# FFN gate tiles copied by DMA into float32r tiles and transposed in that type, with a later flip in the loop

## The chip, the cores and the metric

The kernel runs on one core of one Trainium2 chip, as one launch. The metric is the device time of a run in microseconds; the runs shown are the median of three. A profile is one execution recorded by the hardware profiler. TensorE (PE, with its weight loads as PEld) multiplies and transposes, VectorE (DVE) and ScalarE (ACT) work element by element, GpSimd (POOL) does small arithmetic and can issue DMAs, SyncE (SP) issues DMAs.

## The reference

A trunk of four residual layers over 256 tokens of 1024 numbers. Each layer has a token mixer (retention, a convolution module, dilated attention, retention again), then a SwiGLU feed-forward part. The change lies in the latter:

```python
def _swiglu(h, w_in, w_out):
    a = h @ w_in
    return (jax.nn.silu(a[..., :FFN_HIDDEN]) * a[..., FFN_HIDDEN:]) @ w_out

for i in range(DEPTH):
    ...                                  # token mixer m
    x = x + _rmsnorm(m, norm_w[i, 1])
    f = _swiglu(_rmsnorm(x, norm_w[i, 2]), ffn_w_in[i], ffn_w_out[i])
    x = x + _rmsnorm(f, norm_w[i, 3])
```

`FFN_HIDDEN` is 2816. All inputs and the output are float32.

## The kernel before

**Precision.** A float32 operand of a large matmul is split into two float32r tiles, a high part and the rest (`split`, lines 50 and 51: ACT casts the high part, DVE subtracts). Three float32r matmuls, high by high, high by rest and rest by high, stand for one float32 product. In the rows, `xTh`/`xTl` are the two parts of the transposed activations, `wh`/`wl` of the weights going up, `poolh`/`pooll` of the weights coming down, `fhh`/`fhl` of the transposed gate tiles.

**Tiling.** The tokens are two halves of 128 (t = 0, 1). The 2816 hidden columns are 11 groups (c) of 256. `proj` (line 183) makes one unit of "up": 24 matmuls of 512 columns (256 gate and 256 value columns) into the PSUM tile `mm`. It is divided into four steps s of 6 matmuls, and its argument `mid` can place other work ahead of a step. ACT then computes the silu of the gate half (line 448) and DVE multiplies it with the value half (line 450), both into the SBUF tile `fsg`.

**Flip.** The product has tokens on the partitions and must have hidden columns there for the next matmul. `flip` (line 459) does this on TensorE: two 128x128 transposes against the identity `ident`, into the PSUM tile `aux`, in float32. Behind it `split` writes `fhh` and `fhl`. `down` (line 200) then has 12 matmuls of 512 columns, which accumulate the output in `acc`. Per layer there are 22 units of up, flip and down, 88 in the kernel.

**Order.** The loop over c is written out by hand: up for group c + 1 of half 0, down for group c of half 0, flip of (0, c + 1), up for group c of half 1, down for group c - 1 of half 1, flip of (1, c). `FFN_HOLD` holds one `down` of half 1 back to the last round. A scheduler then orders the instructions of each engine, and may move a flip by some matmuls. `flush(t)` (line 162) transposes the normalised activations of a half; `finish` adds the result to the residual stream, and POOL computes the root mean squares in it (lines 110 to 113: `rs` of a result, `rsx` of the next input).

**Queues.** All DMAs are issued by SP. Weights come in loads of 512 KB into `raw`, which has 7 buffers. POOL's queue holds only its norm arithmetic. The identity is loaded once, at the start, into a float32 tile.

Of the kernel before, what the change touches and what calls it, by code (L numbers as in the profile page):

```python
# [8 lines left out]
F32 = mybir.dt.float32  # L9
F32R = mybir.dt.float32r  # L10
# [4 lines left out]
P = 128  # L15
# [9 lines left out]
WBUFS = 10  # L25
RAWBUFS = 7
FOBUFS = 6
FFN_HOLD = True
CONV_EARLY = 3
CONV_FENCE = 1  # L30
APE = 3
# [6 lines left out]
def tile_trunk(ctx: ExitStack, tc: tile.TileContext, a):  # L38
    nc = tc.nc

    const = ctx.enter_context(tc.tile_pool(name="const", bufs=1))
    wp = ctx.enter_context(tc.tile_pool(name="wp", bufs=WBUFS))
# [3 lines left out]
    def bank(tag):  # L46
        return ps.tile([P, 512], F32, tag=tag, name=tag, bufs=4 if tag == "acc" else 2)

    def split(h, l, src):
        ia = nc.scalar.copy(h, src)  # L50
        iv = nc.vector.tensor_sub(l, src, h.bitcast(F32))  # L51
        return ia, iv
# [9 lines left out]
    def load_w(src, cols=1024, pool=None, bufs=None):  # L62
        raw = wp.tile([P, 1024], F32, tag="raw", name="raw", bufs=RAWBUFS)
        nc.sync.dma_start(raw[:, :cols], src)
        if pool is None:
            h = wp.tile([P, 1024], F32R, tag="wh", name="wh")
            l = wp.tile([P, 1024], F32R, tag="wl", name="wl")
        else:
            h = pool.tile([P, 1024], F32R, tag="poolh", name="poolh", bufs=bufs)
            l = pool.tile([P, 1024], F32R, tag="pooll", name="pooll", bufs=bufs)  # L70
        cast[0], cast[1] = split(h[:, :cols], l[:, :cols], raw[:, :cols])
        return h, l
# [13 lines left out]
    nc.sync.dma_start(grow, a["norm_w"][0:1, :])  # L86
    for hh in range(2):
        nc.sync.dma_start(xs[0][:, hh * 512 : hh * 512 + 512], a["x"][0][:, hh * 512 : hh * 512 + 512])
    ident = const.tile([P, P], F32, tag="ident", name="ident")
    nc.sync.dma_start(ident, a["ident"])  # L90
    ones = const.tile([1, P], F32, tag="ones", name="ones")
    nc.vector.memset(ones, 1.0)
    gain0 = [bank("acc"), bank("acc")]
# [58 lines left out]
    def flush(t):  # L152
        if t not in todo:
            return
        xg = todo.pop(t)
        h = const.tile([P, KB, P], F32R, tag=f"xTh{t}", name=f"xTh{t}")
        l = const.tile([P, KB, P], F32R, tag=f"xTl{t}", name=f"xTl{t}")
        for hh in range(2):
            b = bank("aux")
            for k in range(4):  # L160
                kk = 4 * hh + k
                nc.tensor.transpose(b[:, k * P : (k + 1) * P], xg[:, kk * P : (kk + 1) * P], ident)
            split(
                h[:, 4 * hh : 4 * hh + 4, :].rearrange("p k t -> p (k t)"),
                l[:, 4 * hh : 4 * hh + 4, :].rearrange("p k t -> p (k t)"),
                b,
            )
        xTh[t], xTl[t] = h, l

    def proj(t, ws, width, out, mid=None):  # L170
        n = 0
        for s in range(4):
            if isinstance(mid, dict):
                if s in mid:
                    mid[s]()
            elif s == 2 and mid is not None:
                mid()
            wh, wl = ws[s]
            for kb in range(2):
                k = 2 * s + kb  # L180
                sl = slice(kb * width, (kb + 1) * width)
                for st, mv in ((xTh, wh), (xTh, wl), (xTl, wh)):
                    nc.tensor.matmul(out, lhsT=st[t][:, k, :], rhs=mv[:, sl], start=(n == 0), stop=(n == 23))  # L183
                    n += 1

    def out_block(acc, sth, stl, w, first, last, by_half=False):
        if by_half:
            for hh in range(2):
                for i, (st, mv) in enumerate(((sth, w[0]), (sth, w[1]), (stl, w[0]))):
                    nc.tensor.matmul(  # L190
                        acc[hh],
                        lhsT=st,
                        rhs=mv[:, hh * 512 : hh * 512 + 512],
                        start=(first and i == 0),
                        stop=(last and i == 2),
                    )
            return
        for i, (st, mv) in enumerate(((sth, w[0]), (sth, w[1]), (stl, w[0]))):
            for hh in range(2):
                nc.tensor.matmul(  # L200
                    acc[hh],
                    lhsT=st,
                    rhs=mv[:, hh * 512 : hh * 512 + 512],
                    start=(first and i == 0),
                    stop=(last and i == 2),
                )
# [228 lines left out]
    def ffn_first(i):  # L435
        return [load_w(a["ffn_w_in"][i, 0, s]) for s in range(4)]
# [3 lines left out]
    def ffn(i, finish, pool):  # L440
        st = {}
        acc = {}

        def up(t, c, mid=None):
            b = bank("mm")
            proj(t, st["w", c], 512, b, mid)
            sg = pool.tile([P, 256], F32, tag="fsg", name="fsg", bufs=3)
            nc.scalar.activation(sg, b[:, 0:256], AF.Silu, scale=rsx[t])  # L448
            sm = sg
            nc.vector.scalar_tensor_tensor(  # L450
                out=sm, in0=b[:, 256:512], scalar=rsx[t], in1=sg, op0=ALU.mult, op1=ALU.mult
            )
            st["s", t, c] = sm

        def flip(t, c):
            sm = st["s", t, c]
            tp = bank("aux")
            for k in range(2):
                nc.tensor.transpose(tp[:, k * P : (k + 1) * P], sm[:, k * P : (k + 1) * P], ident)  # L459
            hh = pool.tile([P, 2, P], F32R, tag="fhh", name="fhh", bufs=4)  # L460
            hl = pool.tile([P, 2, P], F32R, tag="fhl", name="fhl", bufs=4)
            split(hh.rearrange("p a b -> p (a b)"), hl.rearrange("p a b -> p (a b)"), tp[:, 0:256])
            st["h", t, c] = (hh, hl)

        def down(t, c, mid=None):
            if c == 0:
                acc[t] = [bank("acc"), bank("acc")]
            hh, hl = st["h", t, c]
            for k in range(2):
                if k and mid is not None:  # L470
                    mid()
                out_block(
                    acc[t],
                    hh[:, k, :],
                    hl[:, k, :],
                    st["o", c][k],
                    c == 0 and k == 0,
                    c == FFN_GROUPS - 1 and k == 1,
                    by_half=(t == 1 and c == FFN_GROUPS - 1 and k == 1),
                )  # L480

        def wload(c):
            st["w", c] = [load_w(a["ffn_w_in"][i, c, s]) for s in range(4)]

        def oload(c):
            st["o", c] = [load_w(a["ffn_w_out"][i, 2 * c + k], pool=pool, bufs=FOBUFS) for k in range(2)]

        last = FFN_GROUPS - 1
        st["w", 0] = wnext.pop("w") if "w" in wnext else ffn_first(i)
        flush(0)  # L490
        up(0, 0)
        for c in range(FFN_GROUPS):
            if c < last:
                wload(c + 1)
                up(0, c + 1, {1: lambda: flip(0, 0), 2: lambda: flush(1)} if c == 0 else None)
            oload(c)
            down(0, c)
            if c < last:
                flip(0, c + 1)
            up(1, c)  # L500
            if c == last:
                finish(0, acc[0])
            if c == 1:
                flip(1, 0)
            if c == last and FFN_HOLD:
                down(1, c - 2)
            if c >= 1:
                if c != last - 1 or not FFN_HOLD:
                    down(1, c - 1, (lambda: flush(0)) if c == last else None)
                flip(1, c)  # L510
        down(1, last)
        finish(1, acc[1])

# [337 lines left out]
    for i in range(DEPTH):  # L851
# [3 lines left out]
        def finish(t, f):  # L855
            post_norm(t, f, gains[0])
            pre_norm(t, gains[1])
# [26 lines left out]
        with tc.tile_pool(name=f"ffn{i}", bufs=2) as pool:  # L884
            ffn(i, finish_ffn, pool)
# [95 lines left out]
```

## Time and profile before

| | before |
|---|---|
| median of 3 runs | 1611.8 us (1610.49 to 1613.36) |
| profiled execution, its own time | 1612.1 us |
| its span, first to last instruction | 1610.3 us |
| busy share PE / DVE / ACT / POOL | 99% / 64% / 54% / 4% |
| mean granted TensorE clock | 0.997 |
| moved by DMA | 274.27 MB, mean 170 GB/s |

The page shows busy times, the span in slices, DMA queues, the chain of work that ended last, and the costliest groups of instructions. A row of the timeline has the start in us, the length, the engine, the line, the operation, the tile written and the tiles read, shapes and a count; in brackets stands how long the engine sat idle before it and what ended that. The chain lists pieces as start, length, what. `x2` at a piece counts instructions.

### The profile page before, as it was taken

The page shows a single profiled execution, that of the slowest core. Times are in us where ns is not written, and L with a number is a line of the kernel's source. Part 1 is how long each engine was busy: PE and PEld are TensorE (multiplying, and loading weights), DVE is VectorE, ACT ScalarE, POOL GpSimd, SP SyncE. Part 2 cuts the span into 40 slices and gives each one's busy share as a digit, 9 for nine tenths or more (in the row PEclk, how much of TensorE's full clock was granted, in tenths as well). Part 3 has the DMA queues.
Part 4 walks back from the last instruction along what each step waited for, and adds up shares of the span by engine and source line. Part 5 has one row for each costly group of instructions (what it writes and reads, how often), then busy time and mean ns, then how long its engine had stood idle before and what let it go on. Part 6 is the DMA issues. An engine that isn't in the chain of part 4 may idle for free.

```text
span 1610.3 us, 20999 instructions
## 1 busy us (share of the span) xinstructions
PE 1589.4 (99%) x7742; PEld 1344.2 (83%) x7742; DVE 1038.5 (64%) x1576; ACT 864.4 (54%) x1376; POOL 71.3 (4%) x106
## 2 busy tenths in 40 slices
PE   9999999999999999999999999999999999999998
PEld 6888878888787888889999999788888888878886
DVE  7655685646797854567776767755657655675452
ACT  7544464545677644446665656644555444565341
POOL 1000010001000100010000000100011000010000
PEclk9999999999999999999999999999999999999999
DMA  8645465555304755444444444564555554475530
GB/s 315 230 140 186 155 236 184 199 193 183 122 1 138 255 201 191 160 139 144 148 146 139 145 147 158 186 226 164 203 178 166 188 167 138 157 248 194 198 118 27
DMA packets 79881, 274.27 MB, mean 170 GB/s; under 512 B 9377, under 2 KB 9633, under 8 KB 79778
## 3 DMA queue, kind: packets, MB, share of 16 engines
q1 hardware_dynamic: 79778, 272.92, 50.6%
q8 instruction: 61, 1.00, 0.2%
q14 instruction: 42, 0.34, 0.1%
HBM read 271.84 MB, written 1.05 MB: 169 GB/s over the span
## 4 chain that ended last, share of the span: by engine, by line
PE 90%; ACT 3%; DVE 2%; DMA 2%; issue 1%; POOL 1%; SPq 0%; DVEq 0%; POOLq 0%; ACTq 0%
PE mm L183 57%; PE acc L200 21%; PE acc L577 3%; PE acc L774 1%; PE aux L459 1%; PE aux L324 1%; PE acc L733 1%; PE acc L731 1%; PE aux L759 1%; ACT wh L50 1%; ACT junk L118 1%; DMA raw<-in_ffn_w_out 1%; DVE wl L51 1%; PE aux L300 1%; PE aux L695 1%
## 5 line engine op out<-in xcount | busy, mean ns | idle before, releaser
L183 PE MATMUL mm<-wh,xTh 128*128 128x512 f32 (+1 forms) x1536 | 591.1, 385 | 1.2 <-ACT xTh L50 1.2
L183 PE MATMUL mm<-wl,xTh 128*128 128x512 f32 (+1 forms) x1536 | 579.4, 377 | 0.0
L183 PE MATMUL mm<-wh,xTl 128*128 128x512 f32 (+1 forms) x1536 | 579.2, 377 | 0.0
L51 DVE TENSOR_TENSOR wl<-raw,wh 128x1024 fp32r<-128x1024 f32 (+1 forms) x432 | 497.3, 1163 | 116.8 <-ACT wh L50 102.9
L50 ACT CAST wh<-raw 128x1024 fp32r<-128x1024 f32 (+1 forms) x432 | 429.6, 1005 | 138.7 <-PE mm L183 103.6
L183 PEld LDWEIGHTS mm<-wh,xTl 128*128 128x128 f32 x1536 | 288.8, 188 | 45.8 <-DVE xTl L51 0.3
L183 PEld LDWEIGHTS mm<-wh,xTh 128*128 128x128 f32 x1536 | 289.0, 188 | 43.4 <-ACT xTh L50 1.6
L183 PEld LDWEIGHTS mm<-wl,xTh 128*128 128x128 f32 x1536 | 289.4, 188 | 41.9 <-DVE wl L51 0.5
L448 ACT ACTIVATE fsg<-mm,rsx 128x256 f32<-128x256 f32 x88 | 41.7, 474 | 169.0 <-PE mm L183 168.9
L450 DVE SCALAR_TENSOR_TENSOR fsg<-mm,rsx,fsg 128x256 f32<-128x256 f32 x88 | 42.3, 481 | 124.8 <-ACT fsg L448 124.7
L51 DVE TENSOR_TENSOR pooll<-raw,poolh 128x1024 fp32r<-128x1024 f32 x88 | 107.3, 1222 | 7.7 <-ACT poolh L50 7.0
L200 PE MATMUL acc<-poolh,fhh 128*128 128x512 f32 x344 | 107.6, 393 | 0.5 <-ACT fhh L50 0.5
L200 PE MATMUL acc<-poolh,fhl 128*128 128x512 f32 x344 | 107.2, 392 | 0.0
L200 PE MATMUL acc<-pooll,fhh 128*128 128x512 f32 x344 | 106.0, 389 | 0.0
L50 ACT CAST poolh<-raw 128x1024 fp32r<-128x1024 f32 x88 | 92.6, 1054 | 24.2 <-PE acc L200 14.6
L51 DVE TENSOR_TENSOR fhl<-aux,fhh 128x256 fp32r<-128x256 f32 x88 | 37.0, 421 | 98.6 <-ACT fhh L50 98.6
L50 ACT CAST fhh<-aux 128x256 fp32r<-128x256 f32 x88 | 32.5, 369 | 114.4 <-PE aux L459 114.4
L200 PEld LDWEIGHTS acc<-poolh,fhh 128*128 128x128 f32 x344 | 63.7, 188 | 15.1 <-ACT fhh L50 2.7
L200 PEld LDWEIGHTS acc<-pooll,fhh 128*128 128x128 f32 x344 | 64.6, 188 | 13.5
L200 PEld LDWEIGHTS acc<-poolh,fhl 128*128 128x128 f32 x344 | 64.3, 188 | 13.5
L561 DVE SCALAR_TENSOR_TENSOR cv<-upad,wdw,cv 128x256 f32<-128x256 f32 x143 | 59.5, 479 | 0.8
L110 POOL TENSOR_SCALAR rs<-ss 128x1 f32<-128x1 f32 x16 | 7.3, 455 | 1050.9 <-ACT junk L118 1050.9
(178 smaller groups left out, 1617.6 us busy)
## 6 DMA issues: line engine op xcount, KB each, us to landing
raw<-in_ffn_w_in SPq DMA_DIRECT2D x176, 512.0 KB, 4.9
raw<-in_ret_w_in SPq DMA_DIRECT2D x96, 512.0 KB, 4.8
raw<-in_ffn_w_out SPq DMA_DIRECT2D x88, 512.0 KB, 4.5
raw<-in_attn_w_in SPq DMA_DIRECT2D x96, 384.0 KB, 3.8
raw<-in_ret_w_out SPq DMA_DIRECT2D x32, 512.0 KB, 4.4
raw<-in_conv_w_in SPq DMA_DIRECT2D x16, 512.0 KB, 5.0
gain<-in_norm_w SPq DMA_DIRECT2D x15, 512.0 KB, 5.3
raw<-in_conv_w_out SPq DMA_DIRECT2D x8, 512.0 KB, 4.5
```

What stands on the lines that cost most here:

```text
L50: ia = nc.scalar.copy(h, src)
L51: iv = nc.vector.tensor_sub(l, src, h.bitcast(F32))
L118: nc.scalar.activation(junk, src, AF.Square, scale=scale, accum_out=acc)
L183: nc.tensor.matmul(out, lhsT=st[t][:, k, :], rhs=mv[:, sl], start=(n == 0), stop=(n == 23))
L200: nc.tensor.matmul(acc[hh], lhsT=st, rhs=mv[:, hh * 512 : hh * 512 + 512], start=(first and i == 0), stop=(last and i == 2),)
L300: nc.tensor.matmul(b[:, m * 256 : (m + 1) * 256], lhsT=kt[:, 2 + half, m * P : (m + 1) * P], rhs=qt[:, half, :], start=(n == 0), stop=(n = ...
L324: nc.tensor.matmul(b, lhsT=pt[:, m, t * P : (t + 1) * P], rhs=vt[:, m, :], start=(n == 0), stop=(n == 5))
L448: nc.scalar.activation(sg, b[:, 0:256], AF.Silu, scale=rsx[t])
L450: nc.vector.scalar_tensor_tensor(out=sm, in0=b[:, 256:512], scalar=rsx[t], in1=sg, op0=ALU.mult, op1=ALU.mult)
L459: nc.tensor.transpose(tp[:, k * P : (k + 1) * P], sm[:, k * P : (k + 1) * P], ident)
L561: last_tap["v"] = nc.vector.scalar_tensor_tensor(out=cv, in0=upad[:, cb, w : w + 256], scalar=wdw[:, cb, w : w + 1], in1=cv, op0=ALU.mult, ...
L577: nc.tensor.matmul(pc[:, 0:256], lhsT=dgs[w], rhs=upad[:, cb, w : w + 256], start=(w == 0), stop=(w == TAPS - 1),)
```

## The change

Behind DVE's product, the tile `fsg` is copied by a DMA from SBUF to SBUF into a new float32r tile `fsr`. The DMA is issued by POOL. The bits are the same, only the type of the tile differs. The two transposes of a flip read `fsr` and a float32r identity, and write PSUM as float32r. For this the identity is loaded into a `raw` buffer and cast by DVE; all other transposes use the same tile seen as float32. `fsg` has 2 buffers instead of 3, `fsr` 2.

The flip moves in the loop: the flip of (0, c + 1) goes into the up of (1, c), ahead of its last step, and the flip of (1, c) into the up of (0, c + 2), ahead of its last step; in the last round the flip of (1, 9) goes ahead of step 1 of the up of (1, 10). `FFN_HOLD` is gone, and what it chose is written out. The line numbers behind the identity grow by 2 to 4.

```diff
-    ident = const.tile([P, P], F32, tag="ident", name="ident")
-    nc.sync.dma_start(ident, a["ident"])
+    ident_raw = wp.tile([P, 1024], F32, tag="raw", name="raw", bufs=RAWBUFS)
+    nc.sync.dma_start(ident_raw[:, :P], a["ident"])
+    identr = const.tile([P, P], F32R, tag="ident", name="ident")
+    nc.vector.tensor_copy(identr, ident_raw[:, :P])
+    ident = identr.bitcast(F32)
...
-            sg = pool.tile([P, 256], F32, tag="fsg", name="fsg", bufs=3)
+            sg = pool.tile([P, 256], F32, tag="fsg", name="fsg", bufs=2)
...
-            st["s", t, c] = sm
+            smr = pool.tile([P, 256], F32R, tag="fsr", name="fsr", bufs=2)
+            nc.gpsimd.dma_start(smr.bitcast(F32), sm)
+            st["s", t, c] = smr
...
-                nc.tensor.transpose(tp[:, k * P : (k + 1) * P], sm[:, k * P : (k + 1) * P], ident)
+                nc.tensor.transpose(tp[:, k * P : (k + 1) * P].bitcast(F32R), sm[:, k * P : (k + 1) * P], identr)
...
-                up(0, c + 1, {1: lambda: flip(0, 0), 2: lambda: flush(1)} if c == 0 else None)
+                if c == 0:
+                    up(0, 1, {1: lambda: flip(0, 0), 2: lambda: flush(1)})
+                else:
+                    up(0, c + 1, {3: lambda: flip(1, c - 1)})
             oload(c)
             down(0, c)
             if c < last:
-                flip(0, c + 1)
-            up(1, c)
-            if c == last:
+                up(1, c, {3: lambda: flip(0, c + 1)})
+            else:
+                up(1, c, {1: lambda: flip(1, c - 1)})
                 finish(0, acc[0])
-            if c == 1:
-                flip(1, 0)
-            if c == last and FFN_HOLD:
                 down(1, c - 2)
-            if c >= 1:
-                if c != last - 1 or not FFN_HOLD:
-                    down(1, c - 1, (lambda: flush(0)) if c == last else None)
-                flip(1, c)
+            if 1 <= c != last - 1:
+                down(1, c - 1, (lambda: flush(0)) if c == last else None)
+        flip(1, last)
         down(1, last)
```

On PE, in the steady loop, this is what stands around a flip. Before (mm rows are matmuls of an up, acc rows with x2 two matmuls of a down, aux rows the two transposes of a flip):

```order
L200 MATMUL acc<-poolh,fhh 128x512 x2
L200 MATMUL acc<-pooll,fhh 128x512 x2
L200 MATMUL acc<-poolh,fhl 128x512 x2
L459 MATMUL aux<-ident,fsg 128x128 x2
L183 MATMUL mm<-wh,xTh_1951 128x512
L183 MATMUL mm<-wl,xTh_1951 128x512
L183 MATMUL mm<-wh,xTl_1952 128x512
```

And after:

```order
L185 MATMUL mm<-wl,xTh_1785 128x512
L185 MATMUL mm<-wh,xTl_1786 128x512
L463 MATMUL aux<-ident,fsr 128x128 x2
L185 MATMUL mm<-wh,xTh_1785 128x512
L185 MATMUL mm<-wl,xTh_1785 128x512
L185 MATMUL mm<-wh,xTl_1786 128x512
```

The flip left the border between a down and an up, and stands inside an up, 6 matmuls from its end. On POOL, which had only norm arithmetic, the copies come in. At the end of the first FFN, before:

```order
L110 TENSOR_SCALAR rsx<-ss 128x1
L113 TENSOR_TENSOR rsx<-rsx,nhalf 128x1
L110 TENSOR_SCALAR rs<-ss 128x1
L113 TENSOR_TENSOR rs<-rs,nhalf 128x1
L110 TENSOR_SCALAR rsx<-ss 128x1
L113 TENSOR_TENSOR rsx<-rsx,nhalf 128x1
```

And after:

```order
L112 TENSOR_SCALAR rsx<-ss 128x1
L115 TENSOR_TENSOR rsx<-rsx,nhalf 128x1
L456 DMA fsr<-fsg 128x256 x21
L112 TENSOR_SCALAR rs<-ss 128x1
L115 TENSOR_TENSOR rs<-rs,nhalf 128x1
L112 TENSOR_SCALAR rsx<-ss 128x1
L115 TENSOR_TENSOR rsx<-rsx,nhalf 128x1
L456 DMA fsr<-fsg 128x256
```

Of the 22 copies of an FFN, 21 go ahead of the norm of half 0 and the last behind it.

More of the change, by code (lines that the diff above doesn't have):

```diff
@@ L27 @@
 FOBUFS = 6
-FFN_HOLD = True
 CONV_EARLY = 3
```

## The prediction

> **What bounds the kernel now.** I read the page's busy times and chain first, then the windows of the four FFN loops, then the chain inside one loop, then the waits at the flips and the ends of the FFNs.
>
> ```profile
> PE 1589.4 (99%) x7742; PEld 1344.2 (83%) x7742; DVE 1038.5 (64%) x1576; ACT 864.4 (54%) x1376; POOL 71.3 (4%) x106
> PE 90%; ACT 3%; DVE 2%; DMA 2%; issue 1%; POOL 1%; SPq 0%; DVEq 0%; POOLq 0%; ACTq 0%
> ```
>
> TensorE carries 90% of the chain that ended last. A window over the first FFN (PE, PEld, DVE, ACT, POOL busy, then the clock, the DMA share and GB/s) and the chain inside a loop (start, us, what) say why:
>
> ```profile
> 250.00:385.00 135.00, 135.00 (x611) 111.14 (x610) 71.48 (x82) 62.23 (x81) 0.00 (x0) 1.00 0.54 187
> ```
>
> ```profile
> 1089.23 0.22 PE aux L459 x2
> 1089.45 5.47 PE mm L183 x24
> 1094.92 2.72 PE acc L200 x12
> ```
>
> PE never idles there, at full clock, with DVE at 53% and DMA at 54%. A unit is 24 up matmuls, 12 down matmuls and a flip: 5.47 + 2.72 + 0.22 = 8.41 us. Whatever shortens a flip on PE shortens the run; whatever makes PE wait lengthens it.
>
> **The transposes.** There are 88 flips (4 layers, 11 groups, 2 token halves) of 2 transposes.
>
> ```profile
> 789.31 0.87 PE aux L759 x8
> 790.19 4.17 PE mm L183 x24
> 794.68 1.42 PE acc L774 x12
> ```
>
> ```profile
> 1594.79 5.45 PE acc L200 x24
> ```
>
> The first row is eight float32 transposes, 0.109 us each; the flip's 0.22 is two of these. The others are float32r matmuls of 384, 256 and 512 columns: 0.174, 0.118 and 0.227 us each, so 0.054 per 128 columns, and 0.064 at 128 columns on that line. No 128-column float32r operation is in the trace. Bounds: at worst it costs as much as the 256-column row (0.118: two make 0.236, a loss of 1.4 us over 88 flips); at best the bare slope (0.054), with the 0.02 that the matmuls behind a flip take over the undisturbed 5.45 also won: 0.22 - 0.108 + 0.02 = 0.132, or 11.6 us. I take 0.064, since three rows lie on that line: 0.22 - 0.128 = 0.092 a flip, **8.1 us won**.
>
> **The new wait.** Call L the time from the end of DVE's product (line 450) to the copy having landed: POOL's issue, the transfer, the signal. Before, a flip needs only the product. In the steady loop PE's order moves as follows. Before (acc rows are down matmuls, x2 a pair; mm rows up matmuls; fsg the product):
>
> ```order
> L200 MATMUL acc<-pooll,fhh 128x512 x2
> L200 MATMUL acc<-poolh,fhl 128x512 x2
> L459 MATMUL aux<-ident,fsg 128x128 x2
> L183 MATMUL mm<-wh,xTh_1951 128x512
> L183 MATMUL mm<-wl,xTh_1951 128x512
> ```
>
> After (fsr is the copy):
>
> ```order
> L185 MATMUL mm<-wl,xTh_1785 128x512
> L185 MATMUL mm<-wh,xTl_1786 128x512
> L463 MATMUL aux<-ident,fsr 128x128 x2
> L185 MATMUL mm<-wh,xTh_1785 128x512
> L185 MATMUL mm<-wl,xTh_1785 128x512
> L185 MATMUL mm<-wh,xTl_1786 128x512
> ```
>
> The flip now stands behind 12 down and 18 up matmuls instead of 12 down.
>
> ```profile
> 275.43 0.48 DVE L450 SCALAR_TENSOR_TENSOR fsg<-mm,rsx,fsg 128x256 f32<-128x256 f32 x1 [3.55 <-ACT fsg L448]
> 277.44 0.38 PE L459 MATMUL aux<-ident,fsg 128*128 128x128 f32 x2
> ```
>
> Slack is 277.44 - 275.91 = 1.53 before, and 18 x 0.227 = 4.09 more after: 5.6 us hide L. The split behind the flip has 6 up and 12 down matmuls or more before its use. The loop pays nothing up to L = 5.6. Two flips per FFN have less: group 0's second (18 matmuls behind its projection, no down in between) and group 9's second (19 behind):
>
> ```profile
> 229.82 10.91 PE mm L183 x48
> ```
>
> ```profile
> 235.97 0.48 DVE L450 SCALAR_TENSOR_TENSOR fsg<-mm,rsx,fsg 128x256 f32<-128x256 f32 x1
> 385.21 0.48 DVE L450 SCALAR_TENSOR_TENSOR fsg<-mm,rsx,fsg 128x256 f32<-128x256 f32 x1
> 385.74 0.44 PE L459 MATMUL aux<-ident,fsg 128*128 128x128 f32 x2
> ```
>
> The first: the projection ends at 229.82 + 10.91/2 = 235.28, the flip comes at 239.37, the product is ready at 236.45: 2.9 us. The second: the flip at 385.74 follows 7 down matmuls, so the projection ended at 384.15; 19 matmuls later is 388.46, against 385.69: 2.8 us. Nothing up to L = 2.8, beyond it 8(L - 2.8).
>
> **Starts of the FFNs.** PE already waits at the first flips:
>
> ```profile
> 222.26 0.41 PE L459 MATMUL aux<-ident,fsg 128*128 128x128 f32 x2 [1.62 <-issue]
> 537.81 0.44 PE L459 MATMUL aux<-ident,fsg 128*128 128x128 f32 x2 [0.34 <-DVE fsg L450]
> 1036.27 0.44 PE L459 MATMUL aux<-ident,fsg 128*128 128x128 f32 x2 [1.71 <-DVE fsg L450]
> 1423.23 0.41 PE L459 MATMUL aux<-ident,fsg 128*128 128x128 f32 x2 [0.17 <-POOL rsx L113]
> 1431.36 0.44 PE L459 MATMUL aux<-ident,fsg 128*128 128x128 f32 x2 [0.80 <-DVE fsg L450]
> ```
>
> The scheduler puts the first flip later in the second projection. First FFN, PE, before and after (xg: the transposes of the second token half):
>
> ```order
> L183 MATMUL mm<-wh,xTh_1783 128x512
> L459 MATMUL aux<-ident,fsg 128x128 x2
> L183 MATMUL mm<-wl,xTh_1783 128x512
> L183 MATMUL mm<-wh,xTl_1784 128x512
> L162 MATMUL aux<-ident,xg 128x128 x4
> ```
>
> ```order
> L185 MATMUL mm<-wl,xTh_1785 128x512
> L463 MATMUL aux<-ident,fsr 128x128 x2
> L164 MATMUL aux<-ident,xg 128x128 x4
> L185 MATMUL mm<-wh,xTl_1786 128x512
> L185 MATMUL mm<-wh,xTh_1785 128x512
> ```
>
> It moved from behind 10 matmuls of that projection to behind 20; in the second and fourth FFN by 10 too, in the third by 4 (20 to 24). Each wait grows by L and shrinks by the matmuls moved ahead: 3(L - 2.27) + (L - 0.91). The 0.80 goes, its flip having 4.09 more. Together 4L - 8.5.
>
> **Ends of the FFNs.** POOL runs its queue in order, and there the last copy stands behind POOL's norm arithmetic. POOL, after, first FFN:
>
> ```order
> L456 DMA fsr<-fsg 128x256 x21
> L112 TENSOR_SCALAR rs<-ss 128x1
> L115 TENSOR_TENSOR rs<-rs,nhalf 128x1
> L112 TENSOR_SCALAR rsx<-ss 128x1
> L115 TENSOR_TENSOR rsx<-rsx,nhalf 128x1
> L456 DMA fsr<-fsg 128x256
> ```
>
> All DMA rows are new; 21 copies go ahead of the norm, the 22nd behind it.
>
> ```profile
> 389.03 0.56 POOL L113 TENSOR_TENSOR rs<-rs,nhalf 128x1 f32<-128x1 f32 x1
> 394.77 2.83 POOL L113 TENSOR_TENSOR rsx<-rsx,nhalf 128x1 f32<-128x1 f32 x1
> 709.43 2.30 POOL L113 TENSOR_TENSOR rsx<-rsx,nhalf 128x1 f32<-128x1 f32 x1
> 1206.39 2.83 POOL L113 TENSOR_TENSOR rsx<-rsx,nhalf 128x1 f32<-128x1 f32 x1
> ```
>
> ```profile
> 398.96 0.38 PE L459 MATMUL aux<-ident,fsg 128*128 128x128 f32 x2
> 714.16 0.38 PE L459 MATMUL aux<-ident,fsg 128*128 128x128 f32 x2
> 1210.59 0.38 PE L459 MATMUL aux<-ident,fsg 128*128 128x128 f32 x2
> ```
>
> POOL is free at 397.60, 711.73 and 1209.22; the flips stand 1.36, 2.43 and 1.37 later. Three waits of L less that: 3L - 5.2. Behind PE's wait queue the last down matmuls and the next layer. The last FFN has no second pair there and pays nothing.
>
> **How long is L?** DMA issues by size, us from issue to landing:
>
> ```profile
> raw<-in_ffn_w_in SPq DMA_DIRECT2D x176, 512.0 KB, 4.9
> out<-x SPq DMA_DIRECT2D x4, 256.0 KB, 2.0
> x<-in_x SPq DMA_DIRECT2D x2, 256.0 KB, 2.7
> chv<-in_conv_ch SPq DMA_DIRECT2D x1, 20.0 KB, 1.6
> ```
>
> No copy inside SBUF and no DMA issued by POOL is shown. Ends: 1.6 (the smallest) and 4.9 (loads queued behind each other). 128 KB lies between the 20 KB and the 256 KB rows, 2.0; POOL's part I take as its unhindered small operation, 0.56. **L = 2.5**. Starts and ends: 7 x 2.5 - 13.7 = **3.8 us lost**. At L = 1.6, with no wait counted below nothing, it would be 0.8 us won; at 4.9, with the 8(L - 2.8), 37 us lost. I take a value near the lower end because the long row is one of loads standing behind other loads of their own queue, and the copies have a queue to themselves, one at a time.
>
> The Trainium skill, DMA: Bandwidth & Descriptors (Anatomy of one DMA, the gpsimd path), gives about 2.0 us fixed plus bytes over 436 GB/s, an estimate of 2.3 us for 128 KB; by it the loss would be 2.6 and the time 1606.6.
>
> **The rest.** The copies add 88 x 128 KB, 11 MB beside 274; weights are cast ahead, so slightly later loads cost nothing; this cover ends if a load outlasts the 7 raw buffers. The identity's cast stands on DVE behind the product of the second row:
>
> ```profile
> 6.18 1.97 PE L162 MATMUL aux<-ident,xg 128*128 128x128 f32 x8
> 6.29 0.69 DVE L141 TENSOR_TENSOR xg<-x,acc 128x512 f32<-128x512 f32 x1 [1.02 <-PE acc L95]
> ```
>
> ```profile
> 8.73 1.07 ACT L50 CAST xTh<-aux 128x512 fp32r<-128x512 f32 x2
> ```
>
> so the first transposes start at about 7.2 instead of 6.18; the first four, half of 1.97, end by 8.2, before ACT takes them at 8.73: nothing. fsg with 2 buffers has a unit of 8.4 us to be read; nothing. SP issues the same loads in the same order.
>
> **Sum:** 1612.1 (the profiled execution; its span is 1610.3, the median of three runs 1611.8) - 8.1 + 3.8 = **1607.8**.
>
> **Rivals.** *Transposes no cheaper.* A float32r weight load takes longer than that of a flip:
>
> ```profile
> L183 PEld LDWEIGHTS mm<-wh,xTh 128*128 128x128 f32 x1536 | 289.0, 188 | 43.4 <-ACT xTh L50 1.6 <-ACT wh L50 0.2
> L459 PEld LDWEIGHTS aux<-ident,fsg 128*128 128x128 f32 x176 | 23.7, 139 | 18.2 <-DVE fsg L450 5.5 <-issue 2.0 <-POOL rsx L113 0.6
> ```
>
> If such loads, 188 against 139 ns, set the pace of two short transposes, the worse bound holds: 1612.1 + 1.4 + 3.8 = 1617.3, slower. Against it: the line through three sizes has no kink. The Trainium skill, TensorE: Matmul & The Clock Gate (LDWEIGHTS), has a load take columns / 1.2 GHz, an estimate of 0.107 us for 128, which speaks for this rival.
>
> *POOL is held while DVE works.* The same POOL operation took 0.56 us and 2.83 us. If half of that delay falls on the copies, L = 3.5: 7 x 3.5 - 13.7 + 8 x 0.7 - 8.1 = +8.3, so 1620.4. It decides from L = 2.95, where 15L - 36.1 eats 8.1. Against it: POOL's slow operations read SBUF through an engine, a copy through DMA. The Trainium skill, SBUF — State Buffer (Who interferes with whom), also says that DVE operations with two SBUF inputs hold up only POOL operations that read SBUF; no run here shows it for an issue.
>
> *In between, no change.* L = 2.9: 6.6 + 0.8 - 8.1 = -0.7, so 1611.4. *Quicker.* L = 2.0: starts -0.4 and ends +1.3 (no wait below nothing), 0.9 - 8.1, so 1604.9.
>
> **Chances.** Forecast 0.38, quicker 0.08, no change 0.22, transposes no cheaper 0.14, POOL held 0.18. 0.2% (3.2 us) is about what a measurement of this kernel tells from no change. Faster: 0.37 + 0.08 = 0.45. Same: 0.22 and the edges of two others, 0.25. Slower: 0.18 + 0.12 = 0.30. Range 1602 to 1621, the forecast's own 1605 to 1610: 1602 leaves out what the quicker case gives with the best transposes, 1621 half of the held one and all that L = 4.9 would bring.
>
> **What would show it.** Two transposes at 0.13 in the chain (0.22 or more: first rival). Landing of the fsr copies near 2 us from issue; idle before the first and the last flip of the first FFN of L - 0.65 and L - 1.36 (L above 3: second rival). No idle at the flips inside the loop; if there is any, L is over 5 and the forecast is wrong by tens of us.

## The result

The changed kernel takes 1648.1 us (median of 4 runs, 1647.3 to 1648.5) against 1611.3 (4 runs, 1610.5 to 1613.4): 1.0226 times as long, 95% interval 1.0208 to 1.0244. The forecast was 1607.8 in a range of 1602 to 1621. The profiled execution's span went from 1610.3 to 1646.3 us, and the mean granted TensorE clock from 0.997 to 0.989.

The page of the kernel after: engine busy times, the chain by engine, and the copies' row among the DMA issues (KB each, median us from issue to landing).

```profile
PE 1597.3 (97%) x7742; PEld 1349.8 (82%) x7742; DVE 1037.1 (63%) x1577; ACT 864.8 (53%) x1376; POOL 110.7 (7%) x194
...
PE 78%; issue 11%; DMA 4%; DVE 3%; ACT 3%; POOL 1%; POOLq 0%; DVEq 0%; ACTq 0%; SPq 0%
...
fsr<-fsg POOLq DMA_DIRECT2D x88, 128.0 KB, 3.5
```

TensorE's share of the chain fell from 90% to 78%; the copies land 3.5 us after their issue. The loop itself stayed as full as before; this is the same window over the first FFN (PE, PEld, DVE, ACT, POOL busy, clock, DMA share, GB/s).

```profile
250.00:385.00 135.00, 135.00 (x613) 111.04 (x612) 70.80 (x80) 62.09 (x80) 8.77 (x16) 1.00 0.59 203
```

The chain inside a loop, after (start, us, what):

```profile
1087.05 2.72 PE acc L202 x12
1089.77 4.08 PE mm L185 x18
1093.85 0.12 PE aux L463 x2
1093.98 1.46 PE mm L185 x6
```

The flip is 0.12 instead of 0.22, but the unit did not become 0.10 shorter: 2.72 + 4.08 + 0.12 + 1.46 = 8.38, and the flips of the first loop are 8.396 us apart (270.59 to 388.13, 14 units) where they were 8.413 apart before (260.62 to 353.16, 11 units).

The time went to the beginnings and ends of the FFNs. Between the ends of DVE's products, taken in order, and at the program's end:

| stretch, four FFNs together | change, us |
|---|---|
| first product to fourth (the start) | +7.2, +8.6, +9.2, +4.8 = +29.8 |
| fourth product to the last but one (the loop) | -1.9 |
| last but one to last (the end) | +3.4 |
| between FFNs, and ahead of the first | +1.1 |
| from the last store's issue to the end of the span | +3.6 |

With -0.1 between the last product and that store this is the span's 36.0, but for rounding. Some of the flips of the changed kernel in PE's timeline (start, us; in brackets the wait ahead and what ended it):

```profile
226.22 0.47 PE L463 MATMUL aux<-ident,fsr 128*128 128x128 f32 x2 [3.89 <-issue]
...
245.36 0.34 PE L463 MATMUL aux<-ident,fsr 128*128 128x128 f32 x2 [1.99 <-DMA fsr<-fsg]
...
397.02 0.37 PE L463 MATMUL aux<-ident,fsr 128*128 128x128 f32 x2 [2.65 <-DMA fsr<-fsg]
...
551.49 0.34 PE L463 MATMUL aux<-ident,fsr 128*128 128x128 f32 x2 [3.75 <-issue]
...
1058.82 0.47 PE L463 MATMUL aux<-ident,fsr 128*128 128x128 f32 x2 [6.31 <-issue]
...
1456.03 0.34 PE L463 MATMUL aux<-ident,fsr 128*128 128x128 f32 x2 [2.94 <-issue]
```

All waits ahead of flips are 29.8 us, 4.6 before; the four first flips carry 16.9, group 0's second ones 7.5, group 9's second ones 5.1, one flip inside a loop 0.3. "issue" at the first flips is the copy too: the product of 226.22 ended at 221.42. After such a wait PE runs at half clock for a while; windows around the first one (columns as above):

```profile
215.00:226.00 11.00, 7.33 (x33) 5.74 (x31) 8.40 (x11) 5.29 (x9) 3.33 (x5) 0.94 0.88 317
226.00:230.00 4.00, 3.78 (x15) 3.32 (x16) 2.16 (x3) 1.43 (x3) 0.00 (x0) 0.50 0.78 286
230.00:234.00 4.00, 4.00 (x16) 3.22 (x16) 1.08 (x2) 0.59 (x1) 0.56 (x1) 0.80 0.38 147
234.00:238.00 4.00, 4.00 (x21) 3.27 (x20) 1.77 (x2) 2.69 (x3) 0.00 (x0) 1.00 0.00 0
```

And two neighbouring copies of the first loop, issued at 265.26 and 274.16: what DMA moved in the 4.1 and 4.5 us behind them (packets, MB, share of the 16 engines; then issues with their landing).

```profile
q0 software_dynamic: 48, 0.13, 7.9%
q1 hardware_dynamic: 2, 0.00, 0.3%
...
fsr<-fsg POOLq DMA_DIRECT2D x1, 128.0 KB, 1.9
...
q1 hardware_dynamic: 389, 1.42, 94.2%
...
raw<-in_ffn_w_in SPq DMA_DIRECT2D x2, 512.0 KB, 5.4
...
fsr<-fsg POOLq DMA_DIRECT2D x1, 128.0 KB, 4.3
```

The copies come in two kinds: 36 of 88 land within 1.9 to 2.1 us, with the 16 engines free, and 43 need 3.8 to 5.3, nearly all of them while weight loads keep the engines busy; the median of 3.5 lies between the two. By the DMA packets in the trace, a packet of a copy takes 0.11 us in either case, but in the quick one above the first starts 1.1 us after the issue and the last ends at 1.6, in the slow one at 2.1 and 4.0: the copy's packets wait beside those of the loads. The loads go out in one burst a group; the second token half's copies fall into it, the first half's in between. The first flip of an FFN, the second half's first and its tenth lie inside such bursts, and these are the places of little slack.

### The profile page after: what moved, and what is told of

Its sections match the earlier page's. It is cut to its first block, busy times and chain, and to the rows that moved or that the text cites. A ratio compares the mean times of both kernels' runs of the same rounds, so it can differ in the third digit from the quotient of the medians.

```text
span 1646.3 us, 21277 instructions
## 1 busy us (share of the span) xinstructions
PE 1597.3 (97%) x7742; PEld 1349.8 (82%) x7742; DVE 1037.1 (63%) x1577; ACT 864.8 (53%) x1376; POOL 110.7 (7%) x194
## 4 chain that ended last, share of the span: by engine, by line
PE 78%; issue 11%; DMA 4%; DVE 3%; ACT 3%; POOL 1%; POOLq 0%; DVEq 0%; ACTq 0%; SPq 0%
PE mm L185 49%; PE acc L202 17%; PE acc L580 3%; DMA fsr<-fsg 2%; PE acc L777 1%; PE aux L326 1%; PE acc L736 1%; PE acc L734 1%; DVE wl L50 1%; PE aux L762 1%; ACT wh L49 1%; ACT junk L120 1%; DMA raw<-in_ffn_w_out 1%; PE aux L463 1%; PE aux L302 1%
## 5 line engine op out<-in xcount | busy, mean ns | idle before, releaser
L456 POOL DMA_DIRECT2D fsr<-fsg x88 | 48.4, 550 | 643.2 <-DVE fsg L452 643.0
L463 PEld LDWEIGHTS aux<-ident,fsr 128*128 128x128 f32 x176 | 24.1, 142 | 45.1 <-issue 27.5
```

The costliest lines, as they stand in the source:

```text
L456: nc.gpsimd.dma_start(smr.bitcast(F32), sm)
L463: nc.tensor.transpose(tp[:, k * P : (k + 1) * P].bitcast(F32R), sm[:, k * P : (k + 1) * P], identr)
```

## The experiments

Theory W: PE's waits for the copies at the places of little slack, and the half clock behind them, are the loss, and a 128-column transpose costs PE nearly the same in either type. Its rivals: O (the later place of the flip costs), C (the chain's 0.10 us a flip is real and something else eats it), D (the copies cost something wherever they stand). On why the copies are late: E (weight loads beside them), F (such a copy takes that long anyhow), Q (POOL's queue is slow). G is against the half clock, T and N are about the program's end. Times are medians, ratios against the kernel before run beside them (1611.7 to 1612.5 us).

**The order alone, and the type alone.** *order_only* is the kernel before with the new loop (a part of the edit):

```
-                flip(0, c + 1)
-            up(1, c)
+                up(1, c, {3: lambda: flip(0, c + 1)})
...
```

> The kernel before with the later flips alone: float32, no copy. Theory W (PE's waits for the copy and the half clock behind them are the loss): without copies nothing is lost; the 0.80 us wait of the fourth FFN goes, the other early waits stay, about 1610.5 us, same as before. Rival O (the later place of the flip costs by itself): 1615 or more.

1610.0 us, 0.9988 (0.9979 to 0.9996). Rival O falls. *direct* is the changed kernel without its copy:

```
-            sm = sg
+            smr = pool.tile([P, 256], F32R, tag="fsr", name="fsr", bufs=2)
             nc.vector.scalar_tensor_tensor(
-                out=sm, in0=b[:, 256:512], scalar=rsx[t], in1=sg, op0=ALU.mult, op1=ALU.mult
+                out=smr, in0=b[:, 256:512], scalar=rsx[t], in1=sg, op0=ALU.mult, op1=ALU.mult
             )
-            smr = pool.tile([P, 256], F32R, tag="fsr", name="fsr", bufs=2)
-            nc.gpsimd.dma_start(smr.bitcast(F32), sm)
```

> The changed kernel with the copies left out: the vector engine writes its product straight into the float32r tile (which rounds it, so the values differ a little), later flips, float32r transposes. Theory W: no waits, and the flip is worth only what the distance between flips shows (8.413 against 8.396 us, 0.017 each, 1.5 us in all): about 1609. Rival C (the chain's 0.22 against 0.12 us a flip is real, 8.8 us in all, and some 7 us are lost elsewhere): about 1602.

1608.0 us, 0.9977 (0.9968 to 0.9986). Float32r transposes without copies are worth some 2 us over order_only, not 8.8, with intervals that still touch; the copies are what cost 40. The chain of order_only shows where the 0.10 stays:

```profile
303.12 4.08 PE mm L183 x18
307.21 0.22 PE aux L459 x2
307.43 1.39 PE mm L183 x6
308.82 2.72 PE acc L200 x12
```

Flip and six matmuls together: 0.22 + 1.39 = 1.61 in float32, 0.12 + 1.46 = 1.58 in float32r. What the flip no longer shows, the matmuls behind it do.

**The price of a transpose.** Both versions again, each flip's pair transposed twice:

```
             for k in range(2):
+                nc.tensor.transpose(tp[:, (k + 2) * P : (k + 3) * P], sm[:, k * P : (k + 1) * P], ident)
+            for k in range(2):
                 nc.tensor.transpose(tp[:, k * P : (k + 1) * P], sm[:, k * P : (k + 1) * P], ident)
```

> The later flips in float32 without a copy, and every flip transposes its two halves twice (the first pair into the unused half of the bank): 176 more float32 transposes. Price by the eight in a row (0.109 us each): 19 us more than with the later flips alone, 1630.

> The same doubling in the version without copies that writes float32r: 176 more float32r transposes of 128 columns. Theory W (a transpose of 128 columns costs PE the same in either type): 19 us more than that version, about 1628. Rival C (0.06 us each, as the line through the longer float32r matmuls and the chain say): 11 us more, about 1613.

1629.9 us, 1.0113 (1.0099 to 1.0126), and 1622.5, 1.0069 (1.0056 to 1.0081). By the medians 176 more transposes cost 19.8 us in float32, 0.113 each, and 14.5 in float32r, 0.083 each: neither 19 nor 11. The chain of direct_twice has the second pair at 0.17, about 0.083 each:

```profile
307.61 0.12 PE aux L461 x2
307.74 0.17 PE aux L463 x2
307.90 1.45 PE mm L185 x6
```

So a float32r transpose among transposes is worth 0.030 less, but the first pair, between 512-column matmuls, only 0.01 each. The Trainium skill, TensorE: Matmul & The Clock Gate (Back-to-back issue gap), has pairs of weight load and matmul settle at about 81 ns for 128 columns; the measured 83 ns agree.

**The places.** *mixed* transposes the three flips of each FFN that seemed to have the least slack in float32 straight from the product, with no copy (the flip makes the same choice):

```
+            smr = sm
+            if (t, c) not in ((0, 0), (1, 0), (1, 9)):
+                smr = pool.tile([P, 256], F32R, tag="fsr", name="fsr", bufs=2)
+                nc.gpsimd.dma_start(smr.bitcast(F32), sm)
```

> The changed kernel without a copy for the 12 flips whose product is needed soonest (the first of each half and the second half's tenth, in each FFN): these are transposed in float32 straight from the product; the other 76 keep copy and float32r. Theory W (the loss is PE's wait at those 12 flips and the half clock behind it): all of the loss goes, about 1609 us. Rival D (the copies delay the weight loads or hold an engine, wherever they stand): well above the kernel before, 1620 or more.

1629.9 us, 1.0117 (1.0100 to 1.0134): half of the loss is gone, and W's 1609 was missed. Taken away at those places, PE's waits appeared at the next ones: up to 1.8 us at the first half's second flip and 3.9, 1.8 and 4.0 at the last flips of three FFNs. There POOL issued the copy late. Timeline of mixed, POOL and PE, third FFN; the product had ended at 1214.18:

```profile
1214.04 2.83 POOL L115 TENSOR_TENSOR rsx<-rsx,nhalf 128x1 f32<-128x1 f32 x1
1216.83 0.62 POOL L458 DMA_DIRECT2D fsr<-fsg  x1
...
1221.87 0.33 PE L468 MATMUL aux<-ident,fsr 128*128 128x128 f32 x2 [4.02 <-DMA fsr<-fsg]
```

*mixed5* takes these two away as well:

```
-            if (t, c) not in ((0, 0), (1, 0), (1, 9)):
+            if (t, c) not in ((0, 0), (0, 1), (1, 0), (1, 9), (1, 10)):
```

> As the run 'mixed', and two more flips of each FFN without a copy: the first half's second and the second half's last, where that run's waits had moved to (0.8 to 4.0 us, the last ones because POOL issued their copies 2.1 to 2.7 us late, behind its own norm arithmetic). 20 of 88 flips are then float32 without a copy. Theory W (all of the loss is PE waiting for copies at places of little slack): 1609 us, as with the later flips alone or 1 us less. Rival D (the copies cost something wherever they stand): 1615 or more.

1612.2 us, 1.0009 (1.0000 to 1.0018). With 68 copies left and none at a place of little slack, it stands 2 us above order_only, and the rest of the loss is gone. These 2 us are at the program's end, as is shown below. W holds on the places; it was wrong about their number.

**Why the copies are late.** *quiet* leaves the FFNs' loads away, but for the first group's. One tile, loaded once, stands in for them, which takes one of the `raw` buffers:

```
-            st["w", c] = [load_w(a["ffn_w_in"][i, c, s]) for s in range(4)]
+            st["w", c] = [load_w(None) for s in range(4)]
...
-            st["o", c] = [load_w(a["ffn_w_out"][i, 2 * c + k], pool=pool, bufs=FOBUFS) for k in range(2)]
+            st["o", c] = [load_w(None, pool=pool, bufs=FOBUFS) for k in range(2)]
```

> The changed kernel with the FFNs' weight loads left out (all but the first group's, which come with the layer ahead): the casts read one constant tile, so the values differ, and the copies have the DMA engines nearly for themselves. Theory E (a copy takes 1.9 us from issue to landing on free DMA engines and 4 to 5 beside a burst of weight loads): nearly every copy lands in about 2 us, the product is ready in its copy 2.5 us later, the waits at the flips fall to 6 us or less, about 1613 us. Rival F (a copy needs its 4 to 5 us anyhow at these places): the waits stay, 1640 or more.

1641.5 us, 1.0182 (1.0167 to 1.0197). The time is F's and not E's. But the copies did land as E said, median and most of them at 1.9 us (page of quiet):

```profile
fsr<-fsg POOLq DMA_DIRECT2D x88, 128.0 KB, 1.9
```

The four first flips still waited 4.0 to 4.3 us. The timeline of quiet (POOL, then DVE) has the other cause; the product ended at 549.94:

```profile
549.79 3.97 POOL L120 TENSOR_TENSOR rsx<-rsx,nhalf 128x1 f32<-128x1 f32 x1
553.72 0.62 POOL L461 DMA_DIRECT2D fsr<-fsg  x1
...
549.85 2.35 DVE L50 TENSOR_TENSOR pooll<-rawc,poolh 128x1024 fp32r<-128x1024 f32 x2
552.12 1.22 DVE L50 TENSOR_TENSOR wl<-rawc,wh 128x1024 fp32r<-128x1024 f32 x1
```

With casts that need not wait for loads, DVE works without a gap, and a POOL operation of one column lasts about as long as the three DVE operations beside it: 3.97 us where it takes 0.56 elsewhere. It stands ahead of the copy, which goes out 3.8 us after the product (2.6 in the third FFN). So *quiet_sp* has SP issue the copies instead:

```
-            nc.gpsimd.dma_start(smr.bitcast(F32), sm)
+            nc.sync.dma_start(smr.bitcast(F32), sm)
```

> As the run 'quiet' (FFN weight loads left out, casts from one constant tile), but the copies are issued by SP, whose queue is then nearly empty, so that neither a burst of loads nor POOL's norm arithmetic stands ahead of them. Theory E (these two are what made 2 to 2.5 us into 4.5 to 6): the first flips come 2.5 us after their product and the time falls to 1612 to 1620. Rival F (something else of the copy is slow at those places): the four first flips still wait 4 us each, 1640.

1618.5 us, 1.0044 (1.0031 to 1.0058), within E's 1612 to 1620. At the first flip the product ended at 224.35 and the flip came 2.51 us later (timeline of quiet_sp); in the third and fourth FFN it was 2.09 and 2.13. In the second it was 3.93, beside a 512 KB load of a norm gain, issued by SP 0.4 us ahead of the copy; these loads are left in.

```profile
223.87 0.48 DVE L457 SCALAR_TENSOR_TENSOR fsg<-mm,rsx,fsg 128x256 f32<-128x256 f32 x1
224.42 0.53 SPq L461 DMA_DIRECT2D fsr<-fsg  x1
...
226.86 0.26 PE L468 MATMUL aux<-ident,fsr 128*128 128x128 f32 x1 [0.55 <-DMA fsr<-fsg]
```

F falls. Of the 6.6 us that quiet_sp stands over the kernel before, some 4 lie outside the FFNs; their cause stays open. *act_queue* is the changed kernel, loads and all, with the copies on the scalar engine (nc.scalar.dma_start):

> The changed kernel with the copies issued by the scalar engine instead of POOL. Theory E (the copy's packets share the 16 DMA engines with the loads whatever queue they come from): the median of the copies beside loads stays at 3.5 us or more, 0 to 0.5 us less for the issue; about 1638 to 1648 us. Rival Q (the software queue of POOL is what is slow): all copies land in about 2 us, about 1612.

1648.8 us, 1.0231 (1.0207 to 1.0255). The copy goes out at once and is late all the same; Q falls. Page and timeline of act_queue (an execution of 1654.0 us; the product ended at 222.43):

```profile
fsr<-fsg ACTq DMA_DIRECT2D x88, 128.0 KB, 3.7
```

```profile
222.47 0.52 ACTq L456 DMA_DIRECT2D fsr<-fsg  x1
...
226.54 0.47 PE L463 MATMUL aux<-ident,fsr 128*128 128x128 f32 x2 [3.14 <-DMA fsr<-fsg]
```

The Trainium skill, DMA: Bandwidth & Descriptors (SWDGE vs HWDGE vs iDMA), has software and hardware queues feed the same 16 engines, which take them in turn. The same lateness from ACT's queue agrees. Why the turns add up to 2 to 3 us a copy no run here shows.

**The half clock.** *warm* puts unneeded transposes where PE waits, and for this fixes the first flip behind 20 matmuls of the second projection (a part of the edit):

```
+            n = {(0, 0): 32, (1, 0): 14}.get((t, c), 0)
+            if n:
+                with tc.issue_after(pe[0].ins):
+                    for k in range(n):
+                        nc.tensor.transpose(tp[:, 384:512], ident, ident)
```

> The changed kernel with filling: 32 float32 transposes of the identity (3.5 us, their results unused) ahead of each FFN's first flip and 14 (1.5 us) ahead of the second half's first, in the time in which PE waits for the copy. Theory W: the flips come no earlier, but PE is not idle and keeps its full clock, so that the 12 us of the half clock are won back: about 1637 us. Rival G (the clock falls there for another cause): no gain, 1648 or a little more.

1650.4 us, 1.0245 (1.0223 to 1.0268). The mean clock did rise, from 0.989 to 0.995, and no time was won. So W's 1637 was missed; G's time came, though not for its reason. From the first product to the fourth the four FFNs took 26.9, 27.2, 27.0 and 25.9 us; in the changed kernel 26.8, 27.8, 26.4 and 25.4. In the first FFN PE was 2.5 us quicker from the first flip to the next one, but the third product came only 1.0 us earlier in that count: its projection ended at about 237.3 (18 matmuls, 4.1 us, ahead of the filling at 241.42), and then ACT's silu and DVE's product each stood behind a weight cast (timeline of warm, ACT, then DVE):

```profile
237.47 1.06 ACT L49 CAST poolh<-raw 128x1024 fp32r<-128x1024 f32 x1 [0.20 <-DMA raw<-in_ffn_w_out]
238.42 0.47 ACT L454 ACTIVATE fsg<-mm,rsx 128x256 f32<-128x256 f32 x1
...
238.56 1.23 DVE L50 TENSOR_TENSOR pooll<-raw,poolh 128x1024 fp32r<-128x1024 f32 x1
239.70 0.48 DVE L456 SCALAR_TENSOR_TENSOR fsg<-mm,rsx,fsg 128x256 f32<-128x256 f32 x1
```

PE then waited longer for the next copy. The half clock is real, and taking most of it away won nothing here, where products and copies are late too. How much it would cost by itself, with nothing else late, stays open.

**What the copies cost where nobody waits.** *unread* is order_only with 88 copies that nobody reads (and 2 buffers of `fsg` instead of 3):

```
+            smr = pool.tile([P, 256], F32R, tag="fsr", name="fsr", bufs=2)
+            nc.gpsimd.dma_start(smr.bitcast(F32), sm)
             st["s", t, c] = sm
```

> The later flips in float32 straight from the product, and all 88 copies made but read by nobody: contention alone. Theory W: 1610 us, the same as the later flips alone. Rival D (copies delay the weight loads or POOL's norm arithmetic): 1615 or more.

1613.2 us, 1.0008 (0.9999 to 1.0017): some 3 us over order_only, though PE's waits at the flips are 2.8 us and the last store is issued at 1604.8 us, in order_only at 1606.1. The difference lies behind that store. The output's DMA rows (first and last issue), with their headers, of the kernels before and after:

```profile
core 0 of [0], span 1610.3 us
...
L882 SPq DMA_DIRECT2D out<-x x4: 332/338/348, 1592.4 to 1607.3; - x4
```

```profile
core 0 of [0], span 1646.3 us
...
L885 SPq DMA_DIRECT2D out<-x x4: 332/340/1468, 1624.7 to 1639.7; - x4
```

From the last issue to the end it is 3.0 us before and 6.6 after; 6.6 in unread, 5.0 in mixed5, 3.0 in order_only. Two more runs, one with `if (i, t, c) == (0, 1, 4):` ahead of the copy and one with nc.scalar.dma_start:

> The later flips alone (float32 from the product), and a single copy on POOL's queue in the first FFN that nobody reads. Every kernel with POOL copies ended 5.0 to 6.6 us after its last store was issued, every one without them 3.0 to 3.1. Theory T (the program's end is longer as soon as POOL has issued any DMA): the end is 5 us or more again and the time about 1612 to 1613 us. Rival N (it grows with the number of copies, or the two runs' 2 to 3 us are the copies' traffic): the end is 3.0 us and the time 1610.

> As the run 'unread' (88 copies that nobody reads), issued by the scalar engine. Theory T: the end is 3.0 to 3.1 us, and the traffic alone costs under 1 us: 1610 to 1611. Rival N (the traffic beside the weight loads costs the 3 us): 1613.

1610.4 us, 0.9990 (0.9981 to 1.0000), and 1609.4, 0.9984 (0.9975 to 0.9993), with ends of 3.2 and 3.1 us. The traffic of 88 copies costs nothing that can be measured, and the longer end belongs to POOL's copies; but one of them is not enough, so T was wrong in that. What takes the time stands in the traces: a DRAIN that POOL runs behind its last work. Its rows in the kernels after, mixed and mixed5 (shortest, median and longest in ns, then first start and last end in us):

```profile
L977 POOLq DRAIN  x3: 34/102/7876, 1637.7 to 1646.1; - x3
...
L982 POOLq DRAIN  x3: 34/102/6896, 1618.6 to 1626.0; - x3
...
L982 POOLq DRAIN  x3: 34/102/6241, 1603.1 to 1609.8; - x3
```

The longest takes 0.67 us where POOL issued no copy, 0.76 with one copy, 6.24 with 68, 6.90 with 76 and 7.88 with 88, whether they are read or not (unread): 0.082 us for each copy. So it is their number that counts, as N had it, and not how late the last ones come.

**The version without copies, once more.** *direct_late* puts direct's first flips later:

```
-                    up(0, 1, {1: lambda: flip(0, 0), 2: lambda: flush(1)})
+                    up(0, 1, {1: lambda: flush(1), 3: lambda: flip(0, 0)})
```

> The version without copies that writes the product as float32r, with each FFN's first flip put behind 12 to 18 instead of some 10 matmuls of the second projection. Its first flips waited 2.5 us in all: 1605.5 us if nothing else becomes late; 1608, as without the move, if the down matmuls then wait for the split.

1608.2 us, 0.9977 (0.9968 to 0.9986), no better than direct: the waits at the flips went to nothing, and others came at the transposes of the second token half (1.6 us). Direct and direct_late both take 0.2% less than the kernel before, with a product rounded to float32r.

## Why the prediction was wrong, step by step

- **L, the step that failed.** "How long is L?" took 2.5 us, because "the copies have a queue to themselves, one at a time". They have a queue, not engines to themselves. At the eleven flips that waited at starts and ends, product to flip was 3.9 to 5.7 us, 4.9 in the mean: the end of the range that the loads' own row had given and that the step set aside. With free engines 2.5 is about right (2.51, 2.09 and 2.13 in quiet_sp; 2.2 for most quick copies of the kernel after, from product to landing). The median of 3.5 would have misled too: the places of little slack got the slow kind. The Trainium skill's figures (DMA: Bandwidth & Descriptors, Anatomy of one DMA), an estimate of 2.3 us, were weighed there too; the 1.9 us of quiet lie near it, the 4 to 5 beside loads do not.
- **The transposes.** 0.12 in the chain was right, the gain of 8.1 us was not: 0.017 a flip by the distances, some 2 us by the runs. The step added up what the chain gives to the flip's own row and not what the unit lost. The rival "transposes no cheaper", a loss of 1.4 us, came nearer, but a small gain is what the runs show.
- **Starts and group 0's second flips.** The formulas were right. With L = 4.9, 4L - 8.5 and four of the eight (L - 2.8) give 11.1 + 8.4 = 19.5 us; the waits grew by 24.4 - 4.6 = 19.8. The starts cost 10 us beyond that, for which the sum had no term: behind five of these waits PE ran some 21 us at half clock. In warm, with all but one of these stretches gone, no time came back. The kernel before had such a stretch too, behind a time in which PE was busy for half of 7 us, and the prediction passed it over (windows of before, columns as above):

```profile
495.00:502.00 7.00, 3.37 (x27) 2.76 (x25) 4.62 (x10) 4.12 (x8) 1.48 (x4) 0.96 0.44 146
502.00:504.00 2.00, 1.82 (x6) 1.54 (x7) 0.69 (x1) 2.00 (x7) 0.00 (x0) 0.50 0.00 0
```

- **Ends.** 3L - 5.2 and four of (L - 2.8) would have been 17.9 us; they cost 3.4. The two were added, though the first wait gives POOL's norm the time that the second was to wait for: mixed, without the first, has the second at up to 4.0. The last FFN has no loads left beside its tenth group, and did not wait there.
- **The loop.** That the loop would pay next to nothing was right: one wait of 0.30 us in 76 flips, with copies landing 1.9 to 5.2 us after their issue. But the cover of 5.6 us holds for the first half's flips alone, from which it was read. The second half's flips, whose copies are the late ones, stand 5.1 to 5.2 us behind their product in nearly all rounds, so the margin was all but used up.
- **The rest.** Traffic for nothing was right (unread_act), the end of the program with POOL's copies, 3.6 us, was not foreseen, and the sum had no term for it. The cast of the identity cost 0.9 us of wait at the start, with no loss to be seen at the first product.
- **The second rival**, POOL held while DVE works, gave a slower kernel, but not for its reason: POOL issued every copy in 0.54 to 0.77 us, in the loops 0.3 after the product. Its mechanism exists (mixed, quiet), on POOL's arithmetic ahead of the copy.

So the sign turned on one number. By the prediction's own formulas L = 4.9 loses 37 us, and with the 2 us of the transposes the time is 1647. That this is close to 1648.1 is luck: the ends are overstated by 14.5 us, and the starts' 10 us and the program's 3.6, which have no term, happen to make up for it.

## What to carry to other kernels

Before putting a transfer on the path, look in the trace at what the DMA engines do at the moment it will be issued, not in the mean: a queue of its own does not keep a copy from waiting behind a burst of loads. Price a shorter instruction by the distance between two units, not by its own row in the chain. And when a few places with little slack carry a loss, expect the wait to move to the next such place when the first is mended.

## What was not expected of the hardware

- A 128 KB copy inside SBUF landed in 1.9 to 2.1 us (36 of 88) or in 3.8 to 5.3 (43), with 9 in between. From issue to landing the DMA share was 0.16 to 0.24 for 35 of those 36, most of it their own packets, and 0.82 or more for 41 of those 43. From ACT's queue it was as late as from POOL's.
- One more transpose of 128 columns in a flip cost 0.083 us in float32r and 0.113 in float32, but the flip's own pair, between 512-column matmuls, only about 0.01 each less in float32r.
- PE ran at half clock behind five waits of 2.2 to 6.3 us (0.50 for the 4 us after 226), not behind one of 2.65 us; with the waits at the starts filled by transposes the mean clock was 0.995 instead of 0.989, at no gain in time.
- With 68 to 88 copies issued by POOL the program ended 5.0 to 6.6 us after its last store's issue, 3.0 to 3.2 with none or one: POOL's drain at the end took 0.082 us more for each copy that POOL had issued.
